# Differential attention on one NeuronCore: transposes issued one by one between score products, and small steps moved from VectorE to ScalarE and GpSimd

## The chip, the cores and the metric

The kernel runs on one NeuronCore of a Trainium2 chip. TensorE (PE) multiplies, VectorE (DVE), ScalarE (ACT) and GpSimd (POOL) do elementwise work, and SyncE (SP) issues the DMAs. The metric is the device time of one execution in microseconds (us), as the median of the timed runs.

## What is computed

One differential-attention layer over 2048 tokens and 256 context tokens, with 1024 features and 8 heads. In the reference (cut):

```python
q, k, v, z = jnp.split(h @ w_in, 4, axis=-1)
s = jnp.einsum('bqhzd,bkhzd->bhzqk', q, k)          # z = 0, 1: two score maps per head
p = jax.nn.softmax(s, axis=-1)
a = p[:, :, 0] - lam * p[:, :, 1]
o = jnp.einsum('bhqk,bkhe->bqhe', a, v)
of = o * lax.rsqrt(jnp.mean(o * o, axis=-1, keepdims=True) + SUBLN_EPS)
y = (of * subln_gain * (1 - lambda_init) * jax.nn.silu(z)) @ w_out
out = rms_norm(x + gate * y, final_gain)
```

All operands are 32-bit floats.

## The kernel before

The program has three stages. `project` forms q, k, v and the gate and writes them to memory (up to about 829 us), `attend` computes the eight heads (829 to 2166 us), and `finish` multiplies by the output matrix and normalises.

`attend` walks through 64 groups: 8 heads of 8 groups, each of 256 queries. A group has two units u of 128 queries, each with two score maps z, and each map is 128 queries by 2304 keys, cut into three chunks of 768. For each chunk `qk` issues four score products of 384 columns into one of two PSUM buffers (`S_BUFS`), and `keep` on DVE scales and copies the chunk to SBUF and takes its minimum. `least` takes the minimum over the chunks. `expo` on ACT takes the exponential of a whole map and its sum. `ratio` on DVE forms the column -lambda * l0 / l1 for the unit, with one reciprocal and one product with two columns. `weigh` on POOL multiplies the second map by that column, and `join` on POOL adds it to the first. Then the joined map is transposed in nine blocks: `turn` issues four transposes of 128x128, `high` on ACT rounds the block to the fast matmul format, `low` on DVE forms the remainder, and `pv` multiplies both with the values in six products of 256 columns. So a group has 12 chunks of scores, 9 blocks of transposes and 9 of value products. `evac`, `clamp`, `square`, `sq_high`, `sq_low` and `sumsq` form the group's sum of squares, and `ssq_out` copies it from PSUM and stores it.

Once per head, when its eight sums of squares are there, they are loaded (`ssq_load`), turned into 16 columns (`ssq_turn`, `ssq_cols`), and `mean` (seven DVE instructions on 128x16) and `root` (two on POOL, a power and a product) form the factor of the norm. `f_turn` and `f_out` turn it back and store it. In the groups of the last head the heads already done are gated too (`last.mul1` on POOL, `last.mul2` and `last.low` on DVE).

The order of the instructions on the four engines is not written out: `Plan.order` computes it. Each step has a nominal cost and a due time, and a free engine takes the step that is due first among those whose inputs and buffers are there. The result is the fixed order in which each engine runs its queue, and an instruction that has to wait holds all that stand behind it on its engine.

The steps that the change and the prediction touch are `qk` (L673), `keep` (L683), `ratio` (L705 and L706), `weigh` (L711), `join` (L715), `turn` (L722), `high` (L730), `low` (L735), `pv` (L744), `ssq_out` (L778), `mean` (L800 to L806), `root` (L809 and L810), and `Plan.order`.

Of the kernel before, what the change touches and what calls it, by code (L numbers as in the profile page):

```python
# [12 lines left out]
F32 = mybir.dt.float32  # L13
# [7 lines left out]
P = 128  # L21
# [85 lines left out]
class Plan:  # L107
    """Orders the instructions of the four engines.

    Every step has an engine, a nominal length, the steps that it reads from, a  # L110
    due time, and the buffers that it takes and gives back.  order() walks
    through time and lets each free engine start the step that is due first
    among those whose inputs and buffers are there.
    """
# [13 lines left out]
    def order(self, look=48):  # L128
# [5 lines left out]
        times = [0.0]  # L134
        while any(queues.values()):
# [7 lines left out]
            for e, queue in queues.items():  # L143
                if free[e] > now + 1e-6:
                    continue
                passed = set()
                for i, s in enumerate(queue[:look]):
                    if s.kind in passed:
                        continue
                    passed.add(s.kind)  # L150
                    if all(d.end is not None and
                           d.end + (0 if d.engine == e else self.HOP[d.engine]) <= now + 1e-6
                           for d in s.deps) and all(have[r] >= s.take.count(r) for r in s.take):
                        for r in s.take:
                            have[r] -= 1
                        s.start, s.end = now, now + s.cost
                        free[e] = s.end
                        for r in s.give:
                            heapq.heappush(back, (s.end + self.HOP[e], r))
                        for t in {0, *self.HOP.values()}:  # L160
                            heapq.heappush(times, s.end + t)
                        queue.pop(i)
                        break
# [14 lines left out]
def project(tc, ph, attend_early, ones, x, ctx, c, c_ctx, norm_gain, ada_w, ada_b, w_in, lam_q, lam_k, subln_gain,  # L178
# [47 lines left out]
    # conditioning  # L226
# [85 lines left out]
    # rms norm, modulation and transposition of a block of tokens  # L312
# [68 lines left out]
    # projections  # L381
# [246 lines left out]
def attend(tc, ph, inner, early, last, ident, ones, mhalf, sums, neglam, q_d, k_d, v_d, o_d, s_d, f_d):  # L628
# [27 lines left out]
    def qk(g, u, z, ck):  # L656
# [6 lines left out]
        if z == 0 and ck == 0:  # L663
            unit[g, u] = SimpleNamespace(p=[], s={}, st=sp.tile([P, 10], F32, tag="st", name=f"st{g}_{u}"))
# [5 lines left out]
        for f in range(2):  # L670
            for b in range(2):
                k0 = ck * CK + b * (CK // 2)
                nc.tensor.matmul(ps[:, b, :CK // 2], group[g].q[:, z, f, u * P:(u + 1) * P],  # L673
                                 head[h].k[:, z, k0:k0 + CK // 2], start=(f == 0), stop=(f == 1))
        if i == NG - 1 and u == G - 1 and z == 1 and ck == NC - 1 and h == H - 2:
# [119 lines left out]
    def mean(h):  # L795
# [32 lines left out]
    for g in range(TOTAL):  # L828
        h = g // NG
        for u in range(G):  # L830
            for z in range(2):
                s0 = g * PER + (u * 2 + z) * NC
                for ck in range(NC):
                    take = ["S"] + (["AB"[z]] if ck == 0 else [])
                    step("qk", "PE", 650, s0 + ck, qk, (g, u, z, ck), take=take)
# [5 lines left out]
            step("ratio", "DVE", 390, due + 1, ratio, (g, u), [("expo", g, u, 0), ("expo", g, u, 1)])  # L841
            step("weigh", "Pool", 2200, due + 2, weigh, (g, u), [("ratio", g, u)])
            step("join", "Pool", 5050, due + 2, join, (g, u), [("weigh", g, u)], give=["B"])
        for b in range(NB):
            due = (g + 1) * PER + LAG + b * PER / NB
            step("turn", "PE", 436, due, turn, (g, b), [("join", g, u) for u in range(G)],
# [307 lines left out]
```

## Time and profile before

| | |
|---|---|
| time, median of 3 runs | 2366.01 us (2363.15 to 2366.03) |
| span of the profiled execution, first to last instruction | 2359.8 us; its time is not listed apart from that, and the span is 6.2 us under the median |
| PE busy | 2251.5 us (95%) |
| DVE busy | 1711.8 us (73%) |
| POOL busy | 1422.9 us (60%) |
| ACT busy | 1220.0 us (52%) |
| DMA, mean share of the 16 engines | 37% |
| mean granted TensorE clock | 0.980 of full speed |

Shares of busy time are over the whole span. What a stage is bound by is read from stretches of it, with the row on which an engine waits.

### The profile page before, as it was taken

How to read it: one execution, taken by the hardware profiler on the slowest of the kernel's cores; microseconds unless marked ns; L12 is line 12 of the kernel's file. 1: busy time of each engine (PE TensorE's matmuls, PEld its weight loads, DVE VectorE, ACT ScalarE, POOL GpSimd, SP SyncE). 2: the span in 40 equal slices, each digit the busy share in tenths (PEclk: the TensorE clock that was granted, in tenths of full speed). 3: DMA queues.
4: the chain of work that ended last, by engine and by line, in shares of the span. 5: the costliest groups of instructions: out<-in, count | busy, mean ns of one | idle time of the engine just before them, and what ended most of it. 6: DMA issues, size and time to landing. Idle time of an engine off the chain costs nothing.

```text
span 2359.8 us, 38159 instructions
## 1 busy us (share of the span) xinstructions
PE 2251.5 (95%) x14353; PEld 2070.0 (88%) x14353; DVE 1711.8 (73%) x3726; ACT 1220.0 (52%) x1717; POOL 1422.9 (60%) x691
## 2 busy tenths in 40 slices
PE   7999999999999989989989989899899899889998
PEld 5988888898888879989989989899899898788777
DVE  5746434453233289999999999999999999995664
ACT  5612312232112167767767767677677676564221
POOL 2523233343223268878878878878788788774643
PEclk9999999999999999999999999999999999899999
DMA  9965645454442251321311412213113114224672
GB/s 309 292 217 194 217 134 183 133 175 144 143 134 98 90 158 35 75 68 40 97 43 35 115 34 65 85 35 75 64 36 90 58 35 117 70 65 172 196 242 102
DMA packets 201166, 275.49 MB, mean 117 GB/s; under 512 B 13469, under 2 KB 147221, under 8 KB 195861
## 3 DMA queue, kind: packets, MB, share of 16 engines
q1 hardware_dynamic: 200980, 273.04, 37.3%
q8 instruction: 113, 1.85, 0.3%
q14 instruction: 73, 0.59, 0.1%
HBM read 184.78 MB, written 88.22 MB: 116 GB/s over the span
## 4 chain that ended last, share of the span: by engine, by line
PE 78%; DVE 12%; DMA 4%; POOL 2%; issue 2%; ACT 1%; SPq 0%; POOLq 0%; ACTq 0%; DVEq 0%
PE s L673 20%; PE po L744 16%; PE t L722 9%; PE py L1003 4%; DVE p L683 3%; DVE lo L735 1%; DVE mk L803 1%; DVE o L944 1%; PE m22vl L431 1%; PE m23vl L431 1%; PE m21vl L431 1%; PE m13vl L431 1%; PE m12vl L431 1%; PE m11vl L431 1%; PE m20vl L431 1%
## 5 line engine op out<-in xcount | busy, mean ns | idle before, releaser
L683 DVE TENSOR_SCALAR_CACHE_REDUCE p<-s 128x768 f32<-128x768 f32 x768 | 725.3, 949 | 92.9 <-PE s L673 88.2
L673 PE MATMUL s<-k,q 128*128 128x384 f32 x3072 | 702.0, 355 | 53.4 <-DVE p L683 51.0
L701 ACT ACTIVATE p<-p,st 128x2304 f32<-128x2304 f32 x256 | 569.7, 2225 | 233.1 <-DVE st L690 233.0
L715 POOL TENSOR_TENSOR p<-p,p 128x2304 f32<-128x2304 f32 x128 | 661.7, 5170 | 10.5
L673 PEld LDWEIGHTS s<-k,q 128*128 128x128 f32 x3072 | 513.3, 192 | 74.0 <-DVE p L683 70.1
L744 PE MATMUL po<-hi,v 128*128 128x256 f32 x2304 | 524.6, 291 | 0.3 <-ACT hi L730 0.2
L711 POOL TENSOR_SCALAR p<-p,st 128x2304 f32<-128x2304 f32 x128 | 282.6, 2208 | 250.8 <-DVE st L706 157.9
L744 PEld LDWEIGHTS po<-hi,v 128*128 128x128 f32 x2304 | 401.0, 192 | 4.5 <-ACT ot L752 2.1
L735 DVE TENSOR_TENSOR lo<-t,hi 128x512 fp32r<-128x512 f32 x576 | 392.9, 684 | 10.6 <-ACT hi L730 9.3
L730 ACT CAST hi<-t 128x512 fp32r<-128x512 f32 x576 | 319.7, 582 | 130.8 <-PE t L722 129.8
L722 PE MATMUL t<-ident,p 128*128 128x128 f32 x2304 | 347.6, 275 | 4.1 <-POOL p L715 4.1
L744 PE MATMUL po<-lo,v 128*128 128x256 f32 x1152 | 329.0, 286 | 14.9 <-DVE lo L735 14.9
L722 PEld LDWEIGHTS t<-ident,p 128*128 128x128 f32 x2304 | 277.9, 142 | 13.6 <-POOL p L715 4.9
L744 PEld LDWEIGHTS po<-lo,v 128*128 128x128 f32 x1152 | 221.7, 192 | 17.0 <-DVE lo L735 16.6
L1003 PE MATMUL py<-wo,gh 128*128 128x512 f32 (+1 forms) x528 | 163.7, 392 | 4.0 <-ACT gh L950 4.0
L1003 PEld LDWEIGHTS py<-wo,gh 128*128 128x128 f32 x528 | 98.7, 189 | 27.1 <-ACT gh L950 4.9
L1003 PE MATMUL py<-wo,gl 128*128 128x512 f32 (+1 forms) x264 | 103.6, 392 | 1.3 <-DVE gl L954 1.3
L950 ACT CAST gh<-o 128x512 fp32r<-128x512 f32 x32 | 19.8, 620 | 106.4 <-DVE o L944 103.4
L940 POOL TENSOR_TENSOR o<-o,f 128x512 f32<-128x512 f32 x32 | 42.8, 1338 | 42.4 <-DMA o<-od 33.4
L1016 POOL TENSOR_TENSOR fv<-fv,fx 128x512 f32<-128x512 f32 x30 | 42.6, 1435 | 39.8 <-DVE fv L1011 36.7
L944 DVE TENSOR_TENSOR o<-o,gate 128x512 f32<-128x512 f32 x32 | 47.2, 1477 | 26.3 <-POOL o L940 26.3
L683 DVE DVE_READ_ACCUMULATOR p<-s 128x1 f32 x768 | 62.4, 81 | 0.0
(592 smaller groups left out, 3936.6 us busy)
## 6 DMA issues: line engine op xcount, KB each, us to landing
q<-qd SPq DMA_DIRECT2D x256, 128.0 KB
k<-kd SPq DMA_DIRECT2D x32, 576.0 KB
v<-vd SPq DMA_DIRECT2D x16, 1152.0 KB
aw<-in_ada_w SPq DMA_DIRECT2D x12, 1024.0 KB
xl<-in_x SPq DMA_DIRECT2D x16, 512.0 KB
wod<-hlwo SPq DMA_DIRECT2D x16, 512.0 KB
od<-ot SPq DMA_DIRECT2D x64, 128.0 KB
o<-od SPq DMA_DIRECT2D x32, 256.0 KB
```

What stands on the lines that cost most here:

```text
L431: nc.tensor.matmul(tiles["m", nm][:, t * 256:(t + 1) * 256], tok[:, j, ts], ww[:, j], start=(i == 0), stop=(i == 3 * NCH - 1))
L673: nc.tensor.matmul(ps[:, b, :CK // 2], group[g].q[:, z, f, u * P:(u + 1) * P], head[h].k[:, z, k0:k0 + CK // 2], start=(f == 0), stop=(f = ...
L683: nc.vector.tensor_scalar(un.p[z][:, ck * CK:(ck + 1) * CK].rearrange("p (b k) -> p b k", b=2), un.s[z, ck][:, :, :CK // 2], -0.125, None, ...
L701: nc.scalar.activation(un.p[z], un.p[z], AF.Exp, bias=un.st[:, 6 + z:7 + z], scale=-1.0, accum_out=acc)
L711: nc.gpsimd.tensor_scalar(p[1], p[1], unit[g, u].st[:, 9:10], 1.0, op0=ALU.mult, op1=ALU.mult)
L715: nc.gpsimd.tensor_tensor(p[0], p[0], p[1], op=ALU.add)
L722: nc.tensor.transpose(pt[:, (e * G + u) * P:(e * G + u + 1) * P], unit[g, u].p[0][:, kt * P:(kt + 1) * P], ident)
L730: nc.scalar.copy(t[1], t[0])
L735: nc.vector.tensor_tensor(t[2], t[0], f32(t[1]), op=ALU.subtract)
L744: nc.tensor.matmul(po, head[h].v[:, vi, kt], tt[:, e * GQ:(e + 1) * GQ], start=(kt == 0 and n == 0), stop=(kt == KT - 1 and n == 2))
L944: self.nc.vector.tensor_tensor(t.o, t.o, t.gate, op=ALU.mult)
L1003: nc.tensor.matmul(py[r, i], aa[:, ts], w[h][:, f, sl], start=(h == 0 and n == 0), stop=(h == H - 1 and n == 2))
```

## The change

There are six edits, all in `Plan.order` and `attend`.

1. `qk` and `turn` become generators that give way after each matmul. `Plan.order` pairs a `turn` with a `qk` that follows it closely on PE, prefers such partners by a due time that is up to 4 slots earlier, and the emitting loop takes one matmul of each in turn.
2. `ratio` keeps the reciprocal alone. The product of lambda and l0 becomes a step on ACT (`lam_l0`), and `weigh` multiplies by both columns.
3. The seven DVE instructions of `mean` become one reciprocal, due earlier, and seven POOL instructions at the head of `root`.
4. `ssq_out` copies on ACT instead of DVE.
5. `lam_exp` and `lam_join` are planned first.
6. Nominal costs: qk 650 to 700, turn 436 to 200, pv 654 to 710, ratio 390 to 165, mean 700 to 250, root 3000 to 4600; new are laml0 with 290, and ssq with 380 on ACT.

```diff
-    def order(self, look=48):
+    def order(self, look=48, pair=None, reach=4.0):
...
+                        ready.append((s.due - (reach if s.kind == want else 0.0), i, s))
...
+                    if e == "PE" and pair:
+                        if s.kind == wanted and now < last.end + 150:
+                            s.after, wanted = last, None
+                        else:
+                            wanted = {pair[0]: pair[1], pair[1]: pair[0]}.get(s.kind)
+                        last = s
...
                 nc.tensor.matmul(ps[:, b, :CK // 2], group[g].q[:, z, f, u * P:(u + 1) * P],
                                  head[h].k[:, z, k0:k0 + CK // 2], start=(f == 0), stop=(f == 1))
+                yield
...
         nc.vector.reciprocal(st[:, 9:10], st[:, 8:9])
-        nc.vector.tensor_scalar(st[:, 9:10], st[:, 9:10], neglam[:, 0:1], l0_col(g, u),
-                                op0=ALU.mult, op1=ALU.mult)
+
+    def lam_l0(g, u):
+        nc.scalar.activation(unit[g, u].st[:, 10:11], l0_col(g, u), AF.Copy, scale=neglam[:, 0:1])
...
-        nc.gpsimd.tensor_scalar(p[1], p[1], unit[g, u].st[:, 9:10], 1.0, op0=ALU.mult, op1=ALU.mult)
+        st = unit[g, u].st
+        nc.gpsimd.tensor_scalar(p[1], p[1], st[:, 9:10], st[:, 10:11], op0=ALU.mult, op1=ALU.mult)
...
                 nc.tensor.transpose(pt[:, (e * G + u) * P:(e * G + u + 1) * P],
                                     unit[g, u].p[0][:, kt * P:(kt + 1) * P], ident)
+                yield
...
-        nc.vector.tensor_copy(row, group[g].m[0:1, :GQ])
+        nc.scalar.copy(row, group[g].m[0:1, :GQ])
...
         nc.vector.reciprocal(hd.r0, hd.l0)
-        nc.vector.scalar_tensor_tensor(hd.u, hd.ssq, 2.0 ** -28, hd.r0, op0=ALU.mult, op1=ALU.mult)
-        nc.vector.scalar_tensor_tensor(hd.u, hd.r0, 2.0 ** -28, hd.u, op0=ALU.mult, op1=ALU.mult)
-        nc.vector.tensor_scalar(hd.mk, hd.u, 2.0 ** 72, None, op0=ALU.is_lt)
-        nc.vector.tensor_scalar(hd.u, hd.u, 2.0 ** 72, 2.0 ** 49, op0=ALU.min, op1=ALU.mult)
-        nc.vector.tensor_scalar(hd.u, hd.u, SUB_EPS, None, op0=ALU.add)
-        nc.vector.tensor_tensor(hd.mk, hd.mk, hd.r0, op=ALU.mult)
 
     def root(h):
+        hd = head[h]
+        nc.gpsimd.tensor_scalar(hd.mk, hd.r0, 2.0 ** -28, 1.0, op0=ALU.mult, op1=ALU.mult)
+        nc.gpsimd.tensor_tensor(hd.u, hd.ssq, hd.mk, op=ALU.mult)
+        nc.gpsimd.tensor_tensor(hd.u, hd.u, hd.mk, op=ALU.mult)
+        nc.gpsimd.tensor_scalar(hd.mk, hd.u, 2.0 ** 72, 1.0, op0=ALU.is_lt, op1=ALU.mult)
+        nc.gpsimd.tensor_scalar(hd.u, hd.u, 2.0 ** 72, 2.0 ** 49, op0=ALU.min, op1=ALU.mult)
+        nc.gpsimd.tensor_scalar(hd.u, hd.u, SUB_EPS, 1.0, op0=ALU.add, op1=ALU.mult)
+        nc.gpsimd.tensor_tensor(hd.mk, hd.mk, hd.r0, op=ALU.mult)
         nc.gpsimd.tensor_tensor(head[h].u, head[h].u, mhalf[:, :n], op=ALU.pow)
         nc.gpsimd.tensor_tensor(head[h].u, head[h].u, head[h].mk, op=ALU.mult)
...
-            step("mean", "DVE", 700, due + 15, mean, (h,), [("scols", h)])
-            step("root", "Pool", 3000, due + 16, root, (h,), [("mean", h)])
+            step("mean", "DVE", 250, due + 12, mean, (h,), [("expo", g, G - 1, 0)])
+            step("root", "Pool", 4600, due + 16, root, (h,), [("mean", h), ("scols", h)])
...
-    for s in plan.order():
-        s.emit()
+    todo = plan.order(pair=("turn", "qk"))
+    held = {id(s.after) for s in todo if s.after}
+    for s in todo:
+        if id(s) in held:
+            continue
+        streams = [r for r in ([s.after.emit()] if s.after else []) + [s.emit()] if r is not None]
+        while streams:
+            for r in list(streams):
+                if next(r, r) is r:
+                    streams.remove(r)
```

The change moves instructions in three places on which the prediction rests. In the rows, a name's first number is the group, s34_0_1_1 is group 34, unit 0, map 1, chunk 1, and t32_6 is block 6 of group 32.

PE, a stretch of group 34, before (L673 scores, L722 transposes, L744 values):

```order
L722 MATMUL t32_6_15264<-ident_125,p0_32_0_14661 128x128
L722 MATMUL t32_6_15264<-ident_125,p0_32_1_14789 128x128
L722 MATMUL t32_6_15264<-ident_125,p0_32_0_14661 128x128
L722 MATMUL t32_6_15264<-ident_125,p0_32_1_14789 128x128
L673 MATMUL s34_0_1_2_15271<-k4_12617,q34_14904 128x384 x4
L744 MATMUL po2_6874<-hi32_4_15240,v4_13114 128x256
```

and now (L688 scores, L740 transposes, L763 values):

```order
L688 MATMUL s34_0_1_1_15257<-k4_12628,q34_14915 128x384
L740 MATMUL t32_6_15259<-ident_125,p0_32_0_14672 128x128
L688 MATMUL s34_0_1_1_15257<-k4_12628,q34_14915 128x384
L740 MATMUL t32_6_15259<-ident_125,p0_32_1_14801 128x128
L688 MATMUL s34_0_1_1_15257<-k4_12628,q34_14915 128x384
L740 MATMUL t32_6_15259<-ident_125,p0_32_0_14672 128x128
L688 MATMUL s34_0_1_1_15257<-k4_12628,q34_14915 128x384
L740 MATMUL t32_6_15259<-ident_125,p0_32_1_14801 128x128
L763 MATMUL po2_6874<-hi32_3_15193,v4_13118 128x256
```

Four transposes in a row have become four that each stand between two score products. Of the 576 blocks, 535 are issued so. A score product comes directly after a transpose 402 times before and 1765 times now.

DVE, where head 3's factor is formed in group 35, before:

```order
L705 RECIPROCAL st34_1_15289<-st34_1_15289 128x1
L706 TENSOR_SCALAR st34_1_15289<-st34_1_15289,neglam_137,l0_4_14654 128x1
L791 COPY ssq3_15484<-ms3_15444 128x16
L800 RECIPROCAL r0_3_15486<-l0_3_12630 128x16
L801 SCALAR_TENSOR_TENSOR u3_15487<-ssq3_15484,r0_3_15486 128x16
L802 SCALAR_TENSOR_TENSOR u3_15487<-r0_3_15486,u3_15487 128x16
L803 TENSOR_SCALAR mk3_15488<-u3_15487 128x16
L804 TENSOR_SCALAR u3_15487<-u3_15487 128x16
L805 TENSOR_SCALAR u3_15487<-u3_15487 128x16
L806 TENSOR_TENSOR mk3_15488<-mk3_15488,r0_3_15486 128x16
L683 TENSOR_SCALAR p0_35_0_15413,st35_0_15412<-s35_0_0_2_15459 128x768
```

and now, near the end of group 34:

```order
L699 TENSOR_SCALAR p1_34_1_15348,st34_1_15301<-s34_1_1_1_15381 128x768
L754 TENSOR_TENSOR lo33_0_15400<-t33_0_15346,hi33_0_15357 128x512
L819 RECIPROCAL r0_3_15414<-l0_3_12640 128x16
L699 TENSOR_SCALAR p1_34_1_15348,st34_1_15301<-s34_1_1_2_15402 128x768
L706 TENSOR_SCALAR st34_1_15301<-st34_1_15301 128x3
```

Seven instructions between two chunk copies have become one, which now stands earlier, near the end of the group before. The six others, as seven, stand on POOL, behind the join of group 34 (L823 to L829), ahead of the power (L830).

ACT, group 33, from the exponential of map 0 on, before:

```order
L701 ACTIVATE p0_33_0_14910,l0_4_14654<-p0_33_0_14910,st33_0_14909 128x2304
L730 CAST hi31_5_15025<-t31_5_14990 128x512
L730 CAST hi31_6_15033<-t31_6_15012 128x512
L701 ACTIVATE p1_33_0_14980,st33_0_14909<-p1_33_0_14980,st33_0_14909 128x2304
L730 CAST hi31_7_15084<-t31_7_15052 128x512
L730 CAST hi31_8_15090<-t31_8_15066 128x512
```

and now:

```order
L717 ACTIVATE p0_33_0_14921,l0_4_14665<-p0_33_0_14921,st33_0_14920 128x2304
L724 ACTIVATE st33_0_14920<-l0_4_14665,neglam_137 128x1
L749 CAST hi31_6_15042<-t31_6_15007 128x512
L749 CAST hi31_7_15046<-t31_7_15028 128x512
L749 CAST hi31_8_15067<-t31_8_15053 128x512
L717 ACTIVATE p1_33_0_14991,st33_0_14920<-p1_33_0_14991,st33_0_14920 128x2304
```

The second exponential now stands behind the cast of block 8, before behind that of block 6.

## Rows read from the trace of the kernel before

**Rows 1.** The page's first line.
```profile
span 2359.8 us, 38159 instructions
```

**Rows 2.** Busy time by stretch: length; PE, PEld, DVE, ACT, POOL; PEclk, DMA, GB/s.
```profile
1241.40:1260.60 19.20, 19.20 (x144) 18.66 (x141) 17.33 (x46) 14.95 (x23) 15.87 (x7) 1.00 0.12 35
1031.10:1059.40 28.30, 21.58 (x145) 20.64 (x144) 26.46 (x57) 15.42 (x22) 18.96 (x9) 0.88 0.09 25
1193.60:1222.40 28.80, 22.07 (x143) 21.15 (x142) 26.34 (x57) 15.29 (x22) 18.87 (x9) 0.88 0.08 24
...
1844.80:1874.00 29.20, 22.43 (x145) 21.51 (x144) 26.45 (x57) 15.51 (x22) 19.00 (x9) 0.82 0.08 23
2021.10:2049.30 28.20, 21.32 (x144) 20.61 (x143) 27.29 (x58) 16.02 (x23) 20.00 (x10) 0.88 0.15 44
2049.30:2072.30 23.00, 20.68 (x142) 20.25 (x141) 22.45 (x49) 15.31 (x23) 17.58 (x8) 0.93 0.24 75
```

**Rows 3.** Timeline of DVE in the stretch from 1193.60 us: start us, length us.
```profile
1198.37 0.24 DVE L800 RECIPROCAL r<-l 128x16 f32<-128x16 f32 x1
1198.65 2.11 DVE L801 SCALAR_TENSOR_TENSOR u<-ssq,r 128x16 f32<-128x16 f32 x1
...
1201.00 4.90 DVE L803 TENSOR_SCALAR mk<-u 128x16 f32<-128x16 f32 x1
```

**Rows 4.** Timeline of POOL in the same stretch.
```profile
1198.54 2.20 POOL L711 TENSOR_SCALAR p<-p,st 128x2304 f32<-128x2304 f32 x1 [0.99 <-DVE ssq L791]
1200.82 5.05 POOL L715 TENSOR_TENSOR p<-p,p 128x2304 f32<-128x2304 f32 x1
```

**Rows 5.** Waits of 1193 to 1223 us: total us, times, longest us.
```profile
PE s L673 <- DVE p L683: 6.7, 1, 6.7
```

**Rows 6.** Timeline of PE in an undisturbed stretch.
```profile
1408.44 0.86 PE L673 MATMUL s<-k,q 128*128 128x384 f32 x4
1409.14 0.28 PE L744 MATMUL po<-hi,v 128*128 128x256 f32 x1
...
1410.56 1.04 PE L722 MATMUL t<-ident,p 128*128 128x128 f32 x8
1411.35 0.95 PE L673 MATMUL s<-k,q 128*128 128x384 f32 x4
1412.14 0.28 PE L744 MATMUL po<-hi,v 128*128 128x256 f32 x1
```

**Rows 7.** Timeline of PE at the single transpose of `f_turn`.
```profile
1056.14 0.27 PE L814 MATMUL pf<-ident,u 128*16 128x128 f32 x1
1056.17 0.36 PE L744 MATMUL po<-hi,v 128*128 128x256 f32 x1
1056.37 0.28 PE L744 MATMUL po<-lo,v 128*128 128x256 f32 x1
1056.49 0.40 PE L744 MATMUL po<-hi,v 128*128 128x256 f32 x2
```

**Rows 8.** Groups of instructions, 820 to 2200 us: busy us, mean ns, idle before.
```profile
L706 DVE TENSOR_SCALAR st<-st,neglam,l 128x1 f32<-128x1 f32 x128 | 34.9, 273 | 4.7
L778 DVE COPY row<-pss 1x256 f32<-1x256 f32 x64 | 25.9, 405 | 4.0 <-PE pss L773 3.8
```

**Rows 9.** Groups of POOL's instructions, 1190 to 1400 us.
```profile
L757 POOL TENSOR_SCALAR sqo<-ot 128x256 f32<-128x256 f32 x10 | 4.0, 400 | 0.9
L810 POOL TENSOR_TENSOR u<-u,mk 128x16 f32<-128x16 f32 x2 | 0.4, 223 | 0.2
```

**Rows 10.** Timeline of ACT in the first stretch of rows 2.
```profile
1242.64 2.25 ACT L701 ACTIVATE p<-p,st 128x2304 f32<-128x2304 f32 x1
1244.77 0.21 ACT L701 ACTIVATION_READ_ACCUMULATOR p<-p,st 128x1 f32 x1
1244.85 0.60 ACT L730 CAST hi<-t 128x512 fp32r<-128x512 f32 x1
```

**Rows 11.** Timeline of DVE in a group of the last head.
```profile
2057.81 4.13 DVE L944 TENSOR_TENSOR o<-o,gate 128x512 f32<-128x512 f32 x1
```

More of the change, by code (lines that the diff above doesn't have):

```diff
@@ L134, in order @@
         times = [0.0]
+        wanted = last = None
         while any(queues.values()):
@@ L146, in order @@
                 passed = set()
+                ready = []
+                want = wanted if e == "PE" else None
                 for i, s in enumerate(queue[:look]):
@@ L153, in order @@
                            for d in s.deps) and all(have[r] >= s.take.count(r) for r in s.take):
[L154 to L163, printed above, removed]
+                        ready.append((s.due - (reach if s.kind == want else 0.0), i, s))
+                        if want is None:
+                            break
+                if ready:
+                    _, i, s = min(ready, key=lambda r: r[:2])
+                    for r in s.take:
+                        have[r] -= 1
+                    s.start, s.end = now, now + s.cost
+                    s.after = None
+                    if e == "PE" and pair:
[4 more added lines that the diff above has]
+                        last = s
+                    free[e] = s.end
+                    for r in s.give:
+                        heapq.heappush(back, (s.end + self.HOP[e], r))
+                    for t in {0, *self.HOP.values()}:
+                        heapq.heappush(times, s.end + t)
+                    queue.pop(i)
         return sorted(self.steps, key=lambda s: (s.start, s.n))
@@ L663, in qk @@
         if z == 0 and ck == 0:
-            unit[g, u] = SimpleNamespace(p=[], s={}, st=sp.tile([P, 10], F32, tag="st", name=f"st{g}_{u}"))
+            unit[g, u] = SimpleNamespace(p=[], s={}, st=sp.tile([P, 11], F32, tag="st", name=f"st{g}_{u}"))
         un = unit[g, u]
@@ L826, in step, with lam_exp, lam_join @@
             kind, engine, cost, due, lambda: fn(*args), [done[d] for d in deps], take, give)
+    def lam_exp():
+        nc.scalar.activation(sums, sums, AF.Exp)
+    def lam_join():
+        nc.vector.tensor_scalar(neglam, sums[:, 1:2], sums[:, 0:1], -LAM_INIT,
+                                op0=ALU.subtract, op1=ALU.add)
+    step("lam1", "Activation", 1400, -1, lam_exp, ())
+    step("lam2", "DVE", 130, 0.6, lam_join, (), [("lam1",)])
     for g in range(TOTAL):
@@ L834, in attend @@
                     take = ["S"] + (["AB"[z]] if ck == 0 else [])
-                    step("qk", "PE", 650, s0 + ck, qk, (g, u, z, ck), take=take)
+                    step("qk", "PE", 700, s0 + ck, qk, (g, u, z, ck), take=take)
                     step("keep", "DVE", 865, s0 + ck + 0.5, keep, (g, u, z, ck), [("qk", g, u, z, ck)],
@@ L840, in attend @@
                 step("expo", "Activation", 2200, due, expo, (g, u, z), [("least", g, u, z)])
-            step("ratio", "DVE", 390, due + 1, ratio, (g, u), [("expo", g, u, 0), ("expo", g, u, 1)])
-            step("weigh", "Pool", 2200, due + 2, weigh, (g, u), [("ratio", g, u)])
+            step("laml0", "Activation", 290, due - 1, lam_l0, (g, u), [("expo", g, u, 0), ("lam2",)])
+            step("ratio", "DVE", 165, due + 1, ratio, (g, u), [("expo", g, u, 1)])
+            step("weigh", "Pool", 2200, due + 2, weigh, (g, u), [("ratio", g, u), ("laml0", g, u)])
             step("join", "Pool", 5050, due + 2, join, (g, u), [("weigh", g, u)], give=["B"])
@@ L845, in attend @@
             due = (g + 1) * PER + LAG + b * PER / NB
-            step("turn", "PE", 436, due, turn, (g, b), [("join", g, u) for u in range(G)],
+            step("turn", "PE", 200, due, turn, (g, b), [("join", g, u) for u in range(G)],
                  take=["T"], give=["A"] * G if b == NB - 1 else [])
@@ L850, in attend @@
             first = [("evac", g - 2)] if b == 0 and g > 1 else []
-            step("pv", "PE", 654, due + 2, pv, (g, b), [("low", g, b)] + first, give=["HI", "LO"])
+            step("pv", "PE", 710, due + 2, pv, (g, b), [("low", g, b)] + first, give=["HI", "LO"])
         due += 2
@@ L858, in attend @@
         step("sumsq", "PE", 220, due + 9, sumsq, (g,), [("sqlow", g)], take=["T"])
-        step("ssq", "DVE", 340, due + 9, ssq_out, (g,), [("sumsq", g)], give=["T"])
+        step("ssq", "Activation", 380, due + 9, ssq_out, (g,), [("sumsq", g)], give=["T"])
         if g % NG == NG - 1:
@@ L868, in attend @@
                 step("f_out", "DVE", 200, due + 18, f_out, (h,), [("f_turn", h)], give=["T"])
-    def lam_exp():
-        nc.scalar.activation(sums, sums, AF.Exp)
-    def lam_join():
-        nc.vector.tensor_scalar(neglam, sums[:, 1:2], sums[:, 0:1], -LAM_INIT,
-                                op0=ALU.subtract, op1=ALU.add)
-    step("lam1", "Activation", 1400, -1, lam_exp, ())
-    step("lam2", "DVE", 130, 4, lam_join, (), [("lam1",)])
     for h in range(H - 1):
```

## The prediction

> **What bounds the kernel now.** I read the page first, for the span [rows 1], and then cut `attend` into stretches of one group each with the view by stretch, because shares over the whole span mix stages. An undisturbed group (the first of the stretches) [rows 2] lasts 19.2 us and PE is busy for all of it; DVE works 17.3, POOL 15.9 and ACT 15.0 us. So PE is the bound, and work taken from the others gains nothing there. Once per head it is different: six groups last 27.8 to 29.3 us (the first two and the last of the six stand in the same view [rows 2]; their mean is 28.7), and the seventh, in the last head, 28.2 against 23.0 of its neighbour. PE is busy only 21 to 22 us of them, and its granted clock averages 0.82 to 0.88: after the wait it runs at its lower level (1.2 instead of 2.4 GHz) for a while.
>
> The timeline of DVE tells why [rows 3]: in `mean`, two instructions on 16 columns took 2.11 and 4.90 us. The timeline of POOL beside it [rows 4] shows the weighing ending at 1200.74 and the join at 1205.87; the two DVE instructions end at 1200.76 and 1205.90. Each waited until POOL's instruction was over. Behind them in DVE's queue stands the next copy of scores, whose PSUM buffer PE needs: PE waited 6.7 us once in that group [rows 5].
>
> In the last head the groups last about 23 us with DVE busy 22.4 (the last of the stretches) [rows 2]: there DVE is the bound, above all by a gated product that took 4.13 us [rows 11].
>
> **The change, part by part.**
>
> The norm's chain (edit 3). Six groups give back 28.7 - 19.2 = 9.5 us each, 57 together, and the seventh 28.2 - 23.0 = 5.2. What is late next in these groups is PE itself. Left on DVE is one reciprocal on 16 columns. It took 0.24 us [rows 3], but at a time when POOL ran nothing, so beside a join it is not shown: between 0.24 us and 0.24 plus a whole wait like the longest, 4.9 us. I take 0.24, since no reciprocal of this kernel is seen to wait, and keep the other end as a rival. On POOL seven instructions on 128x16 are new per head. The nearest rows are 0.22 us for one of that size and 0.40 for 128x256 [rows 9], so 1.6 to 2.8 us per head. POOL has 3.3 us free in a group, and behind them wait a small remainder and the next weighing; if this cover is gone, the transposes of one group start later by at most about 1 us per head. I take 0 and put 7 us into the range.
>
> The product of `ratio` (edit 2) and the copy of the sums (edit 4). DVE loses 2 x 0.273 + 0.405 = 0.95 us per group [rows 8]. In undisturbed groups PE covers that: gain 0. In the seven groups of the last head that are bound by DVE, the instructions behind the gated product count (one product and the copy, 0.68 us, 4.7 in all), while the one ahead of it only lets DVE arrive at the same wait earlier. The bounds are 0, if the gated products wait longer instead, and 7 x 3.5 = 24 us, if they come to lie where POOL is idle. On ACT two scalings of one column are new, between 0.21 us (a read of one column) [rows 10] and 0.41 (the copy that also moves there, at DVE's price) [rows 8], so at most 1.2 us per group on an engine that works 15.0 of 19.2. SP issues the same DMAs; the store of the sums is issued later by at most one exponential, 2.25 us [rows 10], and the next queries, which queue behind on SP, are loaded a whole group ahead.
>
> The order of ACT. The cast of block 8 now stands ahead of the second exponential, so that one waits for PE. I followed one group of the new order. On PE's timeline [rows 6] a block of four scores takes 0.70 us (1408.44 to 1409.14), eight transposes and four scores 1.58, so a transpose 0.11 and a pair of blocks 1.14; six value products take 0.71 (0.12 each [rows 7]). Block 8 comes with the sixth pair, with five pairs, five blocks of values and one of scores ahead of it: 11.09 us at its end. Its cast can start 0.16 later, when the last transpose's record is over (0.27 long, 0.11 before the end), and ends 0.60 later; the exponential and its sum take 2.34 [rows 10], to 14.2. Then the reciprocal (0.24) and a copy (0.95 and 0.08) free a score buffer at 15.5, and PE wants it at 16.0. This is the tightest place that I find, with 0.5 us to spare. So I take no new wait, and put 10 us into the range for small ones.
>
> Transposes and scores by turns (edit 1). What could be hidden is the transpose's 0.11 us. Its price in a row of transposes is the same as alone between a score and a value product: at the single transpose of `f_turn` the values' second product starts 0.23 us after the transpose [rows 7], which is 0.11 for it and 0.12 for a value product. So PE adds the two up whatever stands beside, and 535 x 4 = 2140 transposes moved gain 0. The cost: eight transposes and four scores make 1.58 where 8 x 0.109 + 0.70 = 1.57, so a step from transpose to score costs 0 to 0.01 us, and there are 1765 - 402 = 1363 more of them: 0 to 14 us, and I take 7. The other end is what the value product's start, 0.03 us after the transpose [rows 7], would allow if the rest of the 0.11 could be hidden; it is the first rival.
>
> The Trainium skill (TensorE: Matmul & The Clock Gate, sections on the steps of a matmul and the back-to-back gap) speaks against my zero: weights are loaded ahead of running matmuls, and a matmul of 128 columns then follows after about 56 ns. By that page a transpose between longer products costs 0.056 instead of 0.11 and the edit gains about 115 us, an estimate; the single transpose in the trace took 0.11, and I go by the trace.
>
> Planning lambda first (edit 5) touches the first group alone, and the new nominal costs (edit 6) act through the orders above.
>
> **Sum.** 57 + 5.2 + 4.7 - 7 = 59.9 us less. Against the profiled execution: 2359.8 - 59.9 = 2299.9 us of span. The median of the runs is 6.2 us above that span, which I carry over: 2306 us. Its own range is 2280 (24 instead of 4.7 in the last head, no cost for the steps) to 2325 (14 for the steps, 0 in the last head, and some of the small waits).
>
> **The rivals.**
>
> Transposes hidden. If a transpose costs 0.03, PE needs 2140 x 0.08 = 171 us less, and DVE becomes the bound: 17.3 less 0.95 is 16.4 us in an undisturbed group, and with some tenths of waiting I take 17.0. 53 groups x 2.2 = 117, and the 7 fall away: 2182 us. For it speaks the early start of the product behind a transpose; against it that this product's record is as much longer (0.36 instead of 0.28) and the next one is not earlier. Chance 0.08.
>
> The reciprocal waits for POOL as the two others did. By the same walk it is reached at about 18.9 us of a group, when the join started by the reciprocal of 14.2 (weighing 2.2, join 5.1) runs until about 21.7. DVE stands still for some 3 us, and as PE waited 6.7 where DVE lost 7.0, PE waits nearly all of it: 7 x 2.7 = 19, so 2325 us, up to 2340 if the clock falls too. For it speak the two long waits [rows 3, 4]; against it that its 0.24 us for 16 columns is longer than the other instructions took when free, so it may run in a different manner. The Trainium skill (Advanced Engine Details and Errata, section VectorE Performance Modes) lets an instruction from SBUF to SBUF with even sizes read through both of DVE's ports, and says that the second is shared with GpSimd, so that the two block each other; by that rule the reciprocal on 16 columns would wait. The two long rows agree with the rule, and no row shows a reciprocal beside a join. Chance 0.22.
>
> The pairs hold the scores back. In a pair the last score is issued 0.33 us later (three transposes), so its copy and the buffer come later. From 59.9 / 535 = 0.112 us of wait per pair the gain is used up; if all of the 0.33 reached PE it would be 177 us and the time 2483. Against it speaks the 0.5 us to spare and that no copy is awaited in undisturbed groups. Slower than before: chance 0.05; part of it, a wait under 0.1 us, up to 2355: 0.05.
>
> **How the numbers follow.** The forecast has 0.60, so the time is 2306 us. The range of 2280 to 2338 holds the forecast and most of the waiting reciprocal; outside lie the hidden transposes (0.08), the slower case (0.05), and the upper ends of the others (about 0.07). Within 0.2% (about what a measurement can tell from no change) I put 0.01: gains and waits would have to cancel. Faster has 0.94.
>
> **What would show it.** Right: the long groups are gone from the view by stretch and all last 19.2 to 19.4 us, PE does not wait on `keep`, POOL's seven new instructions take 0.2 to 0.4 us, a pair of blocks takes 1.14 to 1.18 us on PE's timeline. Wrong: pairs of about 0.9 us (transposes hidden); a reciprocal on 128x16 of 2 to 5 us ending with a join; PE waiting on DVE or on a cast in every group.

## The result and the profile after

The changed kernel takes 2321.9 us (median of four runs, 2317.9 to 2331.1), the kernel before 2364.6 in the same comparison: a ratio of 0.983, with a 95% interval from 0.980 to 0.985. The time lies in the stated range of 2280 to 2338, but the forecast was 2306: 38 us of span are gone where 60 were expected. It is close to the 2325 us of the second rival, the waiting reciprocal. Whether for that rival's reason is the first thing to ask of the profile.

The page's first line, and then the view by stretch (columns as in [rows 2]) of four groups of the changed kernel: the one in which a head's factor is now formed, the group behind it, an undisturbed one, and one of the last head.

```profile
span 2321.8 us, 37967 instructions
```

```profile
1187.10:1206.40 19.30, 19.30 (x141) 18.52 (x140) 17.34 (x45) 15.46 (x23) 17.49 (x15) 1.00 0.12 35
1206.40:1227.20 20.80, 20.64 (x153) 19.78 (x152) 18.10 (x45) 15.67 (x23) 17.80 (x8) 1.00 0.11 34
1285.30:1304.80 19.50, 19.34 (x143) 18.39 (x141) 17.27 (x43) 15.62 (x24) 15.49 (x7) 1.00 0.71 156
...
1935.70:1959.20 23.50, 21.41 (x136) 19.17 (x137) 21.29 (x46) 15.02 (x21) 14.94 (x8) 0.93 0.31 85
```

The long groups are gone: 19.3 us at a full clock where [rows 2] had 28.8 at 0.88. But an undisturbed group lasts 19.5 us where it lasted 19.2, and PE, which never stood still there before, is now idle for 0.16 of them. The last head's groups are still far above 20.

With the groups measured on PE's timeline, from the first score product of one to that of the next, the two profiled executions compare so (us; numbered from 0):

| | before | after | difference | forecast |
|---|---|---|---|---|
| the six groups with a head's factor | 172.4 | 115.8 | -56.6 | -57 |
| the 47 others from group 3 to group 55 | 900.7 | 920.8 | +20.1 | about +5, of the 7 for the steps |
| the seven DVE-bound ones, 56 to 62 | 171.6 | 167.8 | -3.8 | -9.9 |
| all else (`project`, groups 0 to 2, group 63, `finish`) | 1115.1 | 1117.4 | +2.3 | 0 |

So the large term was right to half a microsecond, and what is missing was lost where the forecast saw almost nothing: in the undisturbed groups, and in the last head.

**The reciprocal.** The timeline of DVE and that of POOL in the changed kernel, from group 18 into group 19:

```profile
1186.89 0.24 DVE L819 RECIPROCAL r<-l 128x16 f32<-128x16 f32 x1
```

```profile
1184.98 5.17 POOL L733 TENSOR_TENSOR p<-p,p 128x2304 f32<-128x2304 f32 x1
...
1199.24 0.20 POOL L823 TENSOR_SCALAR mk<-r 128x16 f32<-128x16 f32 x1
1199.52 0.22 POOL L824 TENSOR_TENSOR u<-ssq,mk 128x16 f32<-128x16 f32 x1
...
1201.15 0.22 POOL L829 TENSOR_TENSOR mk<-mk,r 128x16 f32<-128x16 f32 x1
```

It runs in the midst of a join, as the rival had it, and takes 0.24 us all the same; so it does for all eight heads, 0.241 to 0.243 us, each time beside a join. The rival is out, though its number was near. POOL's seven instructions take 0.20 to 0.29 us each (only in the last two heads does one of them take 0.46 or 0.53).

**The undisturbed groups.** The waits of PE between 820 and 2160 us name a new one, 46 times, where the kernel before has no wait of transposes for `low` at all:

```profile
PE t L740 <- DVE lo L754: 18.6, 46, 4.2
```

One of them on PE's timeline, and DVE's beside it:

```profile
1447.35 1.04 PE L688 MATMUL s<-k,q 128*128 128x384 f32 x5
1448.55 0.33 PE L740 MATMUL t<-ident,p 128*128 128x128 f32 x1 [0.16 <-DVE lo L754]
1448.63 0.42 PE L688 MATMUL s<-k,q 128*128 128x384 f32 x1
1448.89 0.27 PE L740 MATMUL t<-ident,p 128*128 128x128 f32 x1
```

```profile
1446.72 0.96 DVE L699 TENSOR_SCALAR_CACHE_REDUCE p<-s 128x768 f32<-128x768 f32 x1 [0.64 <-PE s L688]
1447.61 0.08 DVE L699 DVE_READ_ACCUMULATOR p<-s 128x1 f32 x1
1447.72 0.16 DVE L706 TENSOR_SCALAR_CACHE_REDUCE st<-st 128x3 f32<-128x3 f32 x1
1447.81 0.08 DVE L706 DVE_READ_ACCUMULATOR st<-st 128x1 f32 x1
1447.81 0.69 DVE L754 TENSOR_TENSOR lo<-t,hi 128x512 fp32r<-128x512 f32 x1
```

Read it backwards. The transpose at 1448.55 needs a PSUM buffer that `low` gives back, which ends at 1448.50. On DVE, `low` stands behind the copy of a chunk of scores and the minimum; and that copy started only at 1446.72, after DVE had stood idle for 0.64 us waiting for the scores of the last pair. The scores of a pair issued by turns are complete 0.33 us later than those of a block issued whole. Idle time of 0.16 us is less than the loss: from the end of the fifth score product (1447.35 + 1.04 = 1448.39) to the end of the transpose (1448.88) it is 0.49 us, where a transpose otherwise ends 0.11 after its forerunner. The wait costs 0.38 us. In 41 of the 53 groups from 3 to 55 a transpose comes late so, mostly by this much.

### The profile page after: what moved, and what is told of

It reads as the page before. It is cut to its first block, busy times and chain, and to the rows that moved or that the text cites. A ratio compares the mean times of both kernels' runs of the same rounds, so it can differ in the third digit from the quotient of the medians.

```text
span 2321.8 us, 37967 instructions
## 1 busy us (share of the span) xinstructions
PE 2247.2 (97%) x14353; PEld 2033.1 (88%) x14353; DVE 1615.4 (70%) x3486; ACT 1279.4 (55%) x1909; POOL 1445.4 (62%) x747
## 4 chain that ended last, share of the span: by engine, by line
PE 78%; DVE 8%; POOL 5%; DMA 4%; issue 4%; ACT 1%; SPq 0%; POOLq 0%; ACTq 0%; DVEq 0%
PE s L688 20%; PE po L763 15%; PE t L740 10%; PE py L1033 5%; DVE p L699 3%; POOL p L733 2%; DVE lo L754 1%; DMA o<-od 1%; PE m23vl L446 1%; PE m12vl L446 1%; PE m22vl L446 1%; PE m21vl L446 1%; PE m13vl L446 1%; PE m11vl L446 1%; PE m20vl L446 1%
## 5 line engine op out<-in xcount | busy, mean ns | idle before, releaser
L688 PE MATMUL s<-k,q 128*128 128x384 f32 x3072 | 843.2, 389 | 8.3 <-DVE p L699 6.8
L740 PE MATMUL t<-ident,p 128*128 128x128 f32 x2304 | 608.8, 274 | 21.3 <-DVE lo L754 18.6
L688 PEld LDWEIGHTS s<-k,q 128*128 128x128 f32 x3072 | 564.7, 191 | 41.0 <-DVE p L699 15.2
L763 PE MATMUL po<-hi,v 128*128 128x256 f32 x2304 | 537.6, 297 | 0.2
L749 ACT CAST hi<-t 128x512 fp32r<-128x512 f32 x576 | 332.7, 583 | 218.5 <-PE t L740 203.3
L729 POOL TENSOR_SCALAR p<-p,st 128x2304 f32<-128x2304 f32 x128 | 292.3, 2284 | 192.9 <-DVE st L721 147.2
L763 PEld LDWEIGHTS po<-hi,v 128*128 128x128 f32 x2304 | 395.6, 190 | 9.1 <-ACT hi L749 0.4
L740 PEld LDWEIGHTS t<-ident,p 128*128 128x128 f32 x2304 | 318.6, 140 | 42.7 <-DVE lo L754 34.9
L763 PE MATMUL po<-lo,v 128*128 128x256 f32 x1152 | 326.9, 284 | 6.7 <-DVE lo L754 6.7
L763 PEld LDWEIGHTS po<-lo,v 128*128 128x128 f32 x1152 | 219.9, 191 | 9.4 <-DVE lo L754 9.1
L1033 PEld LDWEIGHTS py<-wo,gl 128*128 128x128 f32 x264 | 50.5, 191 | 13.9 <-DVE gl L984 2.6
```

The lines of the kernel that those rows point to most:

```text
L729: nc.gpsimd.tensor_scalar(p[1], p[1], st[:, 9:10], st[:, 10:11], op0=ALU.mult, op1=ALU.mult)
L749: nc.scalar.copy(t[1], t[0])
L763: nc.tensor.matmul(po, head[h].v[:, vi, kt], tt[:, e * GQ:(e + 1) * GQ], start=(kt == 0 and n == 0), stop=(kt == KT - 1 and n == 2))
L1033: nc.tensor.matmul(py[r, i], aa[:, ts], w[h][:, f, sl], start=(h == 0 and n == 0), stop=(h == H - 1 and n == 2))
```

## The experiments

The theory to test: the norm's chain gives what was forecast, and issuing by turns costs some 0.3 us or more in each group, mostly by that wait. The rivals: the chain's seven instructions on POOL cost it, or the scalings and copies that moved to ACT do.

Four kernels take the change apart. The first is the kernel before with edit 3 alone:

```diff
 mean:  nc.vector.reciprocal(hd.r0, hd.l0)
-       nc.vector.scalar_tensor_tensor(hd.u, hd.ssq, 2.0 ** -28, hd.r0, ...)
...
 root:
+       nc.gpsimd.tensor_scalar(hd.mk, hd.r0, 2.0 ** -28, 1.0, op0=ALU.mult, op1=ALU.mult)
...
-step("mean", "DVE", 700, due + 15, mean, (h,), [("scols", h)])
+step("mean", "DVE", 250, due + 12, mean, (h,), [("expo", g, G - 1, 0)])
```

> The kernel before with edit 3 alone (the norm's chain moved, with its due times). Theory A (the gain is this chain, and the other edits cost what is missing): the six long groups end at 19.2 us and the seventh at about 23, 57 + 5 = 62 us less than before, about 2302 us, ratio 0.974, and undisturbed groups stay at 19.15. Theory B (the chain on POOL itself costs what is missing, by holding up the transposes of the group behind it): about 2320, ratio 0.982, with PE waiting for POOL or for low in the group after each chain.

Measured: 2306.1 us, ratio 0.977 (0.975 to 0.980). Theory A in the main: the six groups went from 172.4 to 113.8 us, the last head from 171.6 to 165.8, and undisturbed groups stay at 19.15. A little of theory B is there as well: the three groups behind each chain take 20.6, 18.3 and 19.5 us, together 58.4 where three undisturbed ones take 57.5, so 1 us per head. One edit alone is 13 us (by the two ratios) to 16 us faster than all six together.

The second is the kernel before with edit 1 alone:

```diff
-    for s in plan.order():
-        s.emit()
+    todo = plan.order(pair=("turn", "qk"))
...
-step("qk", "PE", 650, ...)   step("turn", "PE", 436, ...)   step("pv", "PE", 654, ...)
+step("qk", "PE", 700, ...)   step("turn", "PE", 200, ...)   step("pv", "PE", 710, ...)
```

> The kernel before with edit 1 alone (pairs in the order, alternate issue, and the three nominal costs of PE's steps that go with it). Theory A (the alternation costs 0.3 us per group: 0.16 of a wait for low and as much for the steps): 64 x 0.3 = 20 us more than before, about 2384, ratio 1.008, groups of 19.5 us, the long groups still there. Theory B (the loss came from the scalings and copies moved to ACT): groups of 19.15 to 19.25, 2362 to 2370. Theory C (hidden transposes, the rival of the prediction): groups under 18.5.

Measured: 2371.7 us, ratio 1.005 (1.003 to 1.006): slower than before. The groups last 19.55 us, as theory A has them, and nothing is hidden (theory C is out). The 47 other groups lost 26.5 us. That the whole is only 11 us slower has a cause that I had not expected: in the new order PE waits 4.3 us in each long group where it waited 6.7, and the six take 152.5 us together in place of 172.4.

The third is the changed kernel with edit 1 undone, the fourth the changed kernel with its order of blocks, but each block of a pair issued whole:

```diff
-        while streams:
-            for r in list(streams):
-                if next(r, r) is r:
-                    streams.remove(r)
+        for r in streams:
+            for _ in r:
+                pass
```

> The changed kernel with edit 1 undone (no pairs, blocks issued whole, the three old nominal costs of PE's steps); edits 2 to 5 stay. Theory A: the 0.3 us per group go, 2322 - 20 = 2302, groups of 19.15, ratio to before 0.974. Theory B (the loss is of edits 2 and 4): still 2318 to 2325.

> The changed kernel with its order of blocks, but each pair issued as eight transposes and then four score products (or the other way round, as the plan has them) in place of by turns. Theory A (issuing by turns costs, by its steps and by the later end of the first block): the wait for low of 0.16 us and the steps go, groups of 19.15 to 19.2 us, about 2305. Theory B (it is the new order of blocks that costs): groups stay at 19.4 to 19.5, 2317 to 2325.

(A block is four transposes; the eight in the second of the two expectations is a slip.) Measured: 2301.1 us (0.974, interval 0.972 to 0.977) and 2293.0 us (0.971, interval 0.970 to 0.973). Theory A holds in both, but the second run gains 12 us more than it asked for, and is the fastest: with the very order of blocks of the changed kernel, whole blocks in place of turns save 29 us (2321.9 - 2293.0; by the two ratios 27). Undisturbed groups of this run, in the view by stretch:

```profile
1431.40:1450.40 19.00, 19.00 (x143) 18.65 (x142) 17.37 (x44) 15.60 (x24) 15.63 (x7) 1.00 0.72 160
1450.40:1469.40 19.00, 19.00 (x144) 18.61 (x142) 17.37 (x44) 15.89 (x25) 16.08 (x7) 1.00 0.12 36
```

They last 18.97 us (19.06 in every other head): less than the 19.15 (there 19.21) of the kernel before. So that kernel was not waiting for nothing either. Between the ends of its successive score products there is one gap of 0.36 us per group, where the others have 0.175, and the waits of PE's weight loads in four such groups of the kernel before (1443 to 1520 us) name it:

```profile
PEld s L673 <- DVE p L683: 1.0, 4, 0.2
```

It was hidden in what I had called a busy PE. The pairs in the plan's order remove that wait (0.18 us per group); the issue by turns adds 0.51 (19.48 - 18.97), of which 0.38 is the new wait, and the rest the steps. A pair as it stands in each, the changed kernel first:

```profile
1293.88 0.34 PE L688 MATMUL s<-k,q 128*128 128x384 f32 x1
1294.06 0.27 PE L740 MATMUL t<-ident,p 128*128 128x128 f32 x1
1294.09 0.42 PE L688 MATMUL s<-k,q 128*128 128x384 f32 x1
1294.35 0.27 PE L740 MATMUL t<-ident,p 128*128 128x128 f32 x1
...
1294.95 0.36 PE L763 MATMUL po<-hi,v 128*128 128x256 f32 x1
```

```profile
1286.36 0.86 PE L688 MATMUL s<-k,q 128*128 128x384 f32 x4
1287.06 0.60 PE L740 MATMUL t<-ident,p 128*128 128x128 f32 x4
1287.41 0.36 PE L763 MATMUL po<-hi,v 128*128 128x256 f32 x1
```

From the first score to the value product behind the pair it is 1.07 us by turns and 1.05 whole. Nothing is hidden by turns, and 0.02 is lost (0.01 by the medians of some 240 such pairs in each run).

The place of the wait, here without one, in PE's and DVE's timelines of the run with whole blocks:

```profile
1437.06 1.57 PE L688 MATMUL s<-k,q 128*128 128x384 f32 x8
1438.47 0.60 PE L740 MATMUL t<-ident,p 128*128 128x128 f32 x4
```

```profile
1436.10 0.96 DVE L699 TENSOR_SCALAR_CACHE_REDUCE p<-s 128x768 f32<-128x768 f32 x1 [0.26 <-PE s L688]
...
1437.19 0.69 DVE L754 TENSOR_TENSOR lo<-t,hi 128x512 fp32r<-128x512 f32 x1
```

Here `low` ends 0.82 us after the first of these scores starts (1437.19 + 0.69 - 1437.06), and the transposes start 1.41 after it, 0.59 after `low`; in the wait above it was 1.15 and 1.20, 0.05 after `low`. So there were some 0.53 us to spare, and the 0.33 by which scores and `low` come later would alone have fitted in. By turns the first transpose also asks for its buffer earlier, behind five scores in place of eight, which is 0.53 us. The two together, 0.86 less the 0.53 to spare, make 0.33 of the 0.38.

**Is it the lateness of the scores, or the turns?** The next run has no turns, but later scores: in every pair the transposes go first (with whole blocks the scores do in all but some 60 of the 535).

```diff
+        pair = sorted([s.after, s], key=lambda p: p.kind == "qk") if s.after else [s]
+        streams = [r for r in [p.emit() for p in pair] if r is not None]
```

> The changed kernel with whole blocks as in the run with whole blocks, but in every pair the four transposes first and then the four scores. Theory A (what costs is that a pair's last score comes late, so that copy, minimum and low on DVE and with them a buffer of transposes come late): the last score is 0.44 us later than with scores first, 0.11 later than by turns; the wait of transposes for low stays or grows to 0.4 to 0.5 us per group, without the steps: groups of 19.3 to 19.5, about 2315 us. Theory B (turns themselves cost): groups of 18.97 as with whole blocks, about 2293.

Measured: 2342.8 us, ratio 0.991 (0.989 to 0.994), so 50 us behind the run with whole blocks. The same place in PE's and DVE's timelines:

```profile
1457.07 0.85 PE L688 MATMUL s<-k,q 128*128 128x384 f32 x4
1458.39 0.66 PE L740 MATMUL t<-ident,p 128*128 128x128 f32 x4 [0.47 <-DVE lo L754]
```

```profile
1456.56 0.96 DVE L699 TENSOR_SCALAR_CACHE_REDUCE p<-s 128x768 f32<-128x768 f32 x1 [0.81 <-PE s L688]
...
1457.64 0.69 DVE L754 TENSOR_TENSOR lo<-t,hi 128x512 fp32r<-128x512 f32 x1
```

It is the same wait, longer. The first transpose here ends 0.8 us after the score product ahead of it (1458.39 + 0.66 less three times 0.11, against 1457.07 + 0.85); by turns it was 0.49, with scores first 0.11. Undisturbed groups last 18.97, 19.48 and 19.90 us as the last score of a pair comes 0, 0.33 and 0.44 us later. Theory A, by more than it asked for: the last 0.11 costs 0.42 us, nearly as much as the first 0.33. A second wait of 0.2 appears in the group, and the transposes ask for their buffer behind four scores, 0.18 us earlier than by turns: `low` 0.45 later and the transposes 0.70 earlier than with whole blocks, less 0.53 to spare, make 0.62 of the 0.69 found. No turn is needed for the loss. But no run parts the later scores from the earlier transposes, and none gives the transposes a fourth buffer (they have three), so that both count is read from the timelines alone.

**Does the plan know?** Two more runs put the nominal cost of four transposes back at 436 ns, with whole blocks and by turns.

```diff
-step("turn", "PE", 200, ...)
+step("turn", "PE", 436, ...)
```

> Whole blocks in pairs, and the nominal cost of four transposes at 436 ns (what they take by the trace) in place of 200. Theory A (the plan is near the limit of PE whatever its nominal costs): within 4 us of the run with whole blocks, 2289 to 2297. Theory B (a plan with true costs also mends the last head, whose groups take 20 to 28 us): 5 to 15 us less, 2278 to 2288.

> The changed kernel, by turns as it is, but with the nominal cost of four transposes at 436 ns (what they take by the trace) in place of 200, so that the plan knows how long a pair lasts. Theory A (the wait of 0.38 us per group comes from a plan that believes a pair to be shorter than it is): the order changes so that the wait goes and the steps alone are left, groups of 19.1, 2300 to 2308. Theory B (the plan cannot see it, since it takes the blocks of a pair one after the other and the by-turns issue delays the first block's end): groups of 19.4 or more, 2315 to 2330.

Measured: 2294.5 us with whole blocks (0.972, interval 0.968 to 0.975), which is theory A, and 2334.9 by turns (0.989, interval 0.987 to 0.991), which is theory B and 5 us above its end. Groups by turns last 19.7 us, and PE still waits for `low` once in each. A true cost doesn't mend it. Nor does it help with whole blocks: the traced execution of that run, the slowest of its four (2303.4 us), has undisturbed groups of 19.13 to 19.20 us and 165.1 us in the last head, where whole blocks with the cost of 200 have 18.97 to 19.06 and 159.7. The medians can't tell the two apart.

**Why the reciprocal did not wait.** Two runs put the first of POOL's seven instructions back on DVE, right behind the reciprocal, whole or cut in two.

```diff
         nc.vector.reciprocal(hd.r0, hd.l0)
+        nc.vector.tensor_scalar(hd.mk, hd.r0, 2.0 ** -28, 1.0, op0=ALU.mult, op1=ALU.mult)
...
+        for a, b in ((0, n - 1), (n - 1, n)):
+            nc.vector.tensor_scalar(hd.mk[:, a:b], hd.r0[:, a:b], 2.0 ** -28, 1.0, op0=ALU.mult, op1=ALU.mult)
```

> The changed kernel with the first of the seven instructions moved back to DVE: a scaling of 128x16 right behind the reciprocal, which in the changed kernel runs in the midst of POOL's join, with 2.4 to 3.2 us of it left, seven times of eight. Theory A (it depends on the instruction: a scaling from SBUF to SBUF waits where a reciprocal does not): the scaling takes 2 to 3.2 us in each of the seven and ends with the join, the groups become 2 us longer or more. Theory B (what waited before was something else, such as reading columns just written): 0.17 to 0.27 us, and groups as in the changed kernel.

> As the run before, but the scaling is cut into one of 15 columns and one of 1 column. Theory A1 (the wait comes with a wide mode that an odd number of columns does not get): both take about 0.2 us beside the join. Theory A2 (any scaling from SBUF to SBUF waits): the first waits 2 to 3.2 us.

One timed run each, so without an interval: 2351.6 and 2352.7 us, 30 more than the changed kernel for one small instruction per head; 23 of them lie in the six groups (138.8 and 139.3 us together), and some of the rest in a later start of `attend`. DVE and POOL in the first:

```profile
1194.59 0.24 DVE L819 RECIPROCAL r<-l 128x16 f32<-128x16 f32 x1
1194.87 2.95 DVE L820 TENSOR_SCALAR mk<-r 128x16 f32<-128x16 f32 x1
```

```profile
1192.65 5.13 POOL L733 TENSOR_TENSOR p<-p,p 128x2304 f32<-128x2304 f32 x1
```

and in the second:

```profile
1199.19 0.24 DVE L819 RECIPROCAL r<-l 128x16 f32<-128x16 f32 x1
1199.47 3.02 DVE L821 TENSOR_SCALAR mk<-r 128x15 f32<-128x15 f32 x2
```

```profile
1197.28 5.13 POOL L733 TENSOR_TENSOR p<-p,p 128x2304 f32<-128x2304 f32 x1
```

The scaling waits until the join is over (1197.82 against 1197.78), right behind a reciprocal of the same size on the same tile that does not. So theory A: the instruction decides. Of the eight scalings of the first run six waited so; the last two heads' met less of a join and took 1.87 and 0.30. Fifteen columns wait like sixteen: theory A1 is out. The scaling of one column says nothing here, as it comes when the join ends. But not every scaling waits: the product of `ratio` in the kernel before, on one column, took 0.272 to 0.274 us the eight times that it ran beside POOL (twice in a join that had over 1 us left), and no more than 0.276 otherwise. The Trainium skill (Advanced Engine Details and Errata, section VectorE Performance Modes) asks for sizes that are both even, or odd, above one and equal, for the mode that blocks with GpSimd; that agrees with 16, 15 and 1 columns, and the prediction told only half of it. It also left out that the section's table of instructions has this mode for `tensor_scalar`, has none for `tensor_tensor`, and does not list a reciprocal: so the section did not say that the reciprocal would wait, and of the two long rows only the one of 4.90 us is its case. Nearly every scaling of 2.95 us made its group some 4 us longer (23.5 us), since PE waited 2.2 and then ran for a while at its lower clock (0.93 over the group).

**The same cure once more.** The last head's groups are bound by gated products that wait for the join [rows 11]. The last run has whole blocks and issues the seven products that the plan of `attend` places there on POOL:

```diff
-step("gmul2", "DVE", 602, due + 5, last.mul2, (0, h), [("gmul1", 0, h)])
+step("gmul2", "Pool", 1350, due + 5, last.mul2, (0, h, nc.gpsimd), [("gmul1", 0, h)])
```

> The run with whole blocks, and the seven gated products of the last head that stand among the groups (DVE, 4.1 us beside a join, 0.6 nominal) issued on POOL as well. Theory A (they wait for POOL's join as the norm's chain did, and DVE is the bound of these groups): the seven groups go from 159.7 us together towards 7 x 19.3 = 135, 10 to 25 us less than with whole blocks, 2268 to 2283. Theory B (POOL, then with 16 to 18 us per group and two products of 1.3, becomes late and the transposes wait for the join): 2288 to 2300.

Measured: 2292.0 us, ratio 0.972 (0.970 to 0.973), no different from whole blocks alone. The seven groups took 159.4 us in place of 159.7. Theory B gives the time but not the reason: PE waits for POOL nowhere in these groups. With whole blocks alone the seven products took 14.4 us on DVE, 9.6 more than the 0.69 of a free one. Some 6 of these came back in other products of two tiles on DVE: the seven `low` of the gated heads took 11.2 us in place of 10.5, the first of them (3.62, shown below) had taken 4.04 already, and a product of the next plan 6.75 in place of 1.72:

```profile
1909.14 3.62 DVE L983 TENSOR_TENSOR gl<-o,gh 128x512 fp32r<-128x512 f32 x1
```

```profile
2029.11 6.75 DVE L973 TENSOR_TENSOR o<-o,gate 128x512 f32<-128x512 f32 x1 [2.23 <-POOL o L969]
```

The second lasts over POOL's join and over the product behind it. What took the rest of the gain is not shown.

## Why the prediction was right, and where it was wrong

**The norm's chain: right, in mechanism and size.** 57 us forecast, 56.6 found, and 58.6 with this edit alone. The reciprocal was taken at 0.24 us and is 0.24. The seven instructions on POOL take 1.6 us per head, the lower end of the estimate (2.1 from the start of the first to the end of the last). The microsecond that they may cost the transposes of the next groups was named and taken as 0; it is there, 1 us per head.

**The second rival: wrong, though its time was nearly measured.** Its chance of 0.22 rested on the two long waits [rows 3, 4]. They were waits of a product of two tiles and of a comparison (a `TENSOR_SCALAR` like the scaling), and the last runs show that these wait and a reciprocal doesn't. The time alone would have confirmed a false story.

**Issuing by turns: the step that failed.** "So I take no new wait, and put 10 us into the range for small ones." The steps themselves were sized well: 0 to 0.01 us each forecast for 1363 of them, and the pair shows 0.01 to 0.02 for its three or four. A transpose costs 0.11 us between score products as in a row, so hiding had no part in it. The price of 0.056 us from the Trainium skill (TensorE: Matmul & The Clock Gate, section Back-to-back issue gap), with its estimate of 115 us gained, isn't borne out; the same section has about 0.081 us where every matmul of 128 columns loads its weights, which the prediction left out, and that isn't borne out either. But the walk through the new order followed ACT and the score buffers, and found its tightest place there, with 0.5 us to spare. It never asked for the transposes' own buffers, whose release stands behind a copy on DVE that waits for the scores. The mechanism is in part that of the third rival (the last score of a pair 0.33 us later, so its copy too), which had 0.05 in its mild form, and there it was looked for at the wrong buffer. The other part, transposes that ask for their buffer 0.53 us earlier, stood in no rival. Against whole blocks it costs 27 to 29 us, not 7.

**A false premise beside it.** "PE is busy for all of it": the kernel before had a hidden wait of 0.18 us per group. So the third rival's "no copy is awaited in undisturbed groups" was wrong too. The order in pairs removes the wait, which the forecast could not see. The two together, 0.33 us per group, make some 15 of the +20 us in the table; the other 5 are the microsecond per head in the three groups behind each chain (20.7, 19.7 and 18.8 us, together 0.8 to 0.9 more than three undisturbed ones).

That the time lies in the range is partly luck. Without the removed wait it would be some 8 us longer (47 x 0.18), about 2330: beyond the 2325 of the forecast's own range, and inside the stated one only because that was widened for a reciprocal that waits.

**The last head.** 9.9 us were forecast. The chain alone brought 5.8 there for the 5.2 of its step, all edits but the turns 11.5 (165.8 to 160.1 is what edits 2, 4 and 5 add, 5.7 for the 4.7 of theirs). By turns it shrinks to 3.8. The sums agree within 1 us, but that may be chance: a nominal cost alone moved the same groups from 159.7 to 165.1. The whole times of the two runs, 2306.1 and 2301.1, have overlapping intervals, so this part rests on the group lengths of one execution each.

**All else.** The +2.3 us of the table are no effect that can be told from scatter: over the twelve profiled executions the first score product comes 823 to 834 us after the start, with `project` the same in all, and the stretch behind the last one takes 218.7 to 223.6 us.

Of the signs that the prediction set, POOL's 0.2 to 0.4 us (but for two instructions) and the pair of 1.14 to 1.18 (four times 0.29 in the rows above) came true; groups of 19.2 to 19.4 did not, and "PE waiting on DVE in every group" was the sign of a wrong step.

## What to carry to other kernels

On an engine that works in order and charges each instruction its full time, issuing two blocks by turns hides nothing, makes the first of them finish later and has the second ask for its buffer earlier: put whole first the block on which the longer chain waits (here the scores, 0.5 to 0.9 us per group). Before a shared engine is blamed for a small instruction, or cleared of it, look at which instruction it is: beside POOL's long ones a reciprocal was free and a scaling of the same tile waited for the rest of the join. And measure a busy engine from end to end of successive instructions, against the same engine in another order; a wait shorter than the overlap of its records does not show as idle time.

The run with whole blocks in the order of the change, 2293.0 us, beats both kernels: 3% faster than the one before, and 1.2% faster than the change as it was made (intervals of 0.970 to 0.973 and 0.980 to 0.985 against the kernel before).

## What had not been expected of the hardware

That DVE's reciprocal on 128x16 runs beside a join in 0.24 us where a scaling on 128x16 or 128x15 takes 2.95 us, to the join's end, and one on a single column takes its usual 0.27. And that a wait of 0.38 us shows as 0.16 of idle time, and one of 0.19 as none, in a stretch where PE's records overlap.
